# Moving matrix products later in program order in the front of a hybrid attention and retention block

## The chip, the core and the metric

The kernel runs on one core of one Trainium2 chip. The metric is the device time of one execution in microseconds (us). The engines are TensorE (PE in the rows; its weight loads are PEld), VectorE (DVE), ScalarE (ACT), GpSimd (POOL) and SyncE (SP, which issues the transfers).

## What is computed

One layer of an encoder over 1024 rows of 1024 numbers, in float32. Two head groups read the same normalised rows through one projection: windowed attention (8 heads) and retention in both directions (8 heads of width 64, in 8 chunks of 128 rows). Then come an output projection and a gated feed-forward layer. The part that matters here is the retention, cut from the reference:

```python
n = rms_norm(x, attn_norm_w[l])
proj = n @ w_in[l]                        # rq, rk, rv, rg are slices of it
inner = einsum('bhcnd,bhcmd->bhcnm', qc, kc) * dmat
out_inner = einsum('bhcnm,bhcme->bhcne', inner, vc)
kv = einsum('bhcmd,bhcme->bhcde', kc * zeta, vc)
def step(r, kv_c):
    return g_chunk * r + kv_c, r
_, states = lax.scan(step, zeros, kv)     # over the chunks; the other direction flipped
cross = einsum('bhcnd,bhcde->bhcne', qc * xi, states)
ret = rms_norm(fwd + bwd, ret_norm_w)
y_ret = silu(rg) * ret
```

## The kernel before

**Passes and steps.** Each operand of a large product is split into a high and a low part, and three matmuls (`passes`, high by high, high by low, low by high) make one product. In the front a projection is a list `seq` of steps (chunk, row tile, depth slice); `sip()` emits one step, which is three matmuls of 512 columns. A row tile of a chunk has eight steps and one PSUM bank, of which there are three (`MM_BUFS`; the first chunk may take two more). `fill(n)` emits n steps, `need(c, t)` emits steps until tile t of chunk c is complete. Steps are used as filler: the other work of the front waits on VectorE, ScalarE and GpSimd, and the steps put between give TensorE something to do meanwhile. `sip()` also calls for the next weights (a transfer on the SP queue, then a split into high and low by ScalarE and VectorE).

**The loops.** For each of two groups g of four retention heads, first a loop over the eight tiles of keys and values (chunk `A`), then `kv_scan` (the recurrence over chunks, twelve operations on VectorE), then a loop over the eight chunks of queries and gates (chunk `B`). After both come keys and values of the attention (chunk `C`), its queries (`D`), attention, the output projection (`O`) and the feed-forward layer, which the change doesn't touch.

**Keys and values, `kv_phase(g, t, ...)`.** Stage one reads tile t's bank: rotation of the keys, values weighted by the decays (`vz`), and high and low parts of both (`kh`, `kl`, `vh`, `vl`). Stage two is the six matmuls of `a<g><t>pk`, keys by values. Stage three is four copies by ScalarE into `KV`.

**Retention, `ret_phase(g, c, ...)`.** Seven stages, divided by yields:

1. rotation of the queries into `qr` (VectorE; tag `t1`, two buffers) and the gate (ScalarE)
2. four transposes `pt`, then `qkh`, `qkl` and the block-diagonal `bq` (rows `BD<-r..qkh`, `BD<-r..qkl`)
3. `s` (queries by keys, six matmuls), `sd` and `sh`, `c` (queries by states, six matmuls), `sl`, `cx`
4. `i`, the inner products: eight matmuls of 128 columns that read `sh`, `sl` and `vhl`
5. `cx` plus `i`, the sum `Y` of both directions, its square
6. mean of squares (VectorE), reciprocal root `rn` (GpSimd)
7. two products on `Y` (GpSimd); the second reads the gate, which lies in `qr`

`go(gen)` emits one stage, `drain(gen)` all that are left. Between two chunks `states(g, c + 1, ...)` writes the next chunk's states and values.

**Who sets the order.** A planner under the kernel makes the queue of each engine. It takes program order as priority and its own estimate of when operands are ready: if the next instruction in program order isn't ready by that estimate, a later one that is goes first. Once made, each queue runs in its order. Buffers are handed out by tag: a tag with two buffers makes the third tile wait until the first is no longer read.

Lines that the change and the steps below touch: `FILL` (38), `AHEAD` (43), `kv_phase` (stage two at its first yield), `kv_scan`, `states`, `ret_phase`, and the two loops over t and c.

Of the kernel before, what the change touches and what calls it, by code (L numbers as in the profile page):

```python
# [34 lines left out]
       "r_bqh": "a", "r_bql": "ad", "r_sh": "a", "r_sl": "d", "r_y": "d", "r_sq": "a", "r_yn": "p", "r_yg": "p",  # L35
       "q_rope": "d", "k_rope": "d", "q_n": "d", "q_h": "p", "q_l": "dp", "q_T": "a", "p_n": "apap", "p_h": "a",
       "o_c": "a", "o_h": "p", "o_l": "p", "y_h": "a", "m_h": "da"}
FILL = {"A": 2, "Aend": 7, "B1": 2, "B2": 5, "C1": 4, "C2": 4, "D0": 6, "D1": 2, "T1": 3, "O0": 4, "O1": 4, "O2": 3}
SOONER = {"w": -80, "exp": 10, "pass": 0}
EARLY, LATE = (0, 4, 1, 5), (2, 3, 6, 7)  # L40
LEAD = 6
EXTRA = (3, 4)
AHEAD = (7, 7, 6)
DOWN_LEAD = 5
RD_BUFS = 10
FIRST_RAW = 8
# [16 lines left out]
def hymba_block(ctx, tc, x, xT, cst, prm, ffnw, wqkv, wkv, wout, wg, wu, wd, out):  # L63
# [69 lines left out]
    def f32(ap):  # L133
        return ap.bitcast(F32)

    def U(name, tag, dt=F32):
        return up.tile([P, 512], dt, name=name, tag=tag, bufs=SLOTS[tag])
# [4 lines left out]
    def ax_ps(name):  # L142
        return pp.tile([P, 512], F32, name=name, tag="ax", bufs=AX_BUFS)
# [48 lines left out]
    A, B, C, D, O = "a", "b", "c", "d", "o"  # L192
# [57 lines left out]
    def sip():  # L250

        c, t, k = seq[pos[0]]
        per = 2 if c[0] == C else 1
        g = first_granule[c] + k // per
        i = part[0]
        if i == 0:
            while len(W) <= g:
                load_next()
            if c == chunks[0] and t == 0:
                split_x(k, 0)  # L260
            if k == 0:
                banks[c, t] = (ax_ps if c == chunks[0] and t in EXTRA else mm_ps)(f"{c[0]}{c[1]}_{t}")
                begun[0] += 1
        width = 512 // per
        o = (k % per) * width
        lh, ll = (X[:, k, t * P:t * P + P] for X in (X_hi, X_lo))
        rh, rl = (w[:, o:o + width] for w in W[g])
        with sooner("pass"):
            pe.matmul(banks[c, t][:, :width], ll if i == 2 else lh, rl if i == 1 else rh,
                      start=k == 0 and i == 0, stop=k == 7 and i == 2)  # L270
        part[0] = (i + 1) % 3
        if i < 2:
            return
        pos[0] += 1
        if c == chunks[0] and t == 3:
            split_x(k, 1)
        if k == 7:
            done.add((c, t))
        if t == tiles[c][-1] and (k + 1) % per == 0:
            freed[0] = g + 1  # L280
        if not hold[0] and pos[0] % PUMP == 0:
            pump(1)

    def ready():
        if pos[0] >= len(seq):
            return False
        c, t, k = seq[pos[0]]
        if (c[0], t, k // 4) in blocked:
            return False
        return k > 0 or part[0] > 0 or begun[0] - taken[0] < MM_BUFS + (len(EXTRA) if c == chunks[0] else 0)  # L290

    def fill(n):

        n = round(3 * n)
        while n and ready():
            sip()
            n -= 1

    def need(c, t):
        while (c, t) not in done:  # L300
            sip()
        return banks[c, t]

    def took():

        taken[0] += 1
# [14 lines left out]
    def row_rms(t):  # L321
        i = xcount[0] % 8
        xcount[0] += 2
        xv = xs[:, i:i + 2, :]
        nc.sync.dma_start(xv, x[t * P:(t + 1) * P, :].rearrange("p (a c) -> p a c", a=2))
        c = slice(t, t + 1)
        act.activation(xv, xv, AF.Square, accum_out=ssq[:, c])
        dve.tensor_scalar(ssq[:, c], ssq[:, c], 1.0 / DM, EPS, op0=ALU.mult, op1=ALU.add)
        pool.tensor_tensor(rstd[:, c], ssq[:, c], mhalf[:, 0:1], op=ALU.pow)
        dve.tensor_scalar(rstd8[:, c], rstd[:, c], HD ** -0.5, None, op0=ALU.mult)  # L330
        dve.tensor_scalar(e2[:, c], ssq[:, c], EPS * HD, None, op0=ALU.mult)
# [64 lines left out]
    def decay_matrix(g):  # L396

        for fb in range(2):
            for h in range(4):
                hh = 4 * g + h  # L400
                act.activation(dms[:, fb, h, :], ab[:, fb, :], AF.Exp, scale=ld[:, fb, hh:hh + 1])
        dve.tensor_tensor(dms[:, 0], dms[:, 0], dms[:, 1], op=ALU.mult)

    def kv_phase(g, t, ps, kr, rv, KV):

        n = f"a{g}{t}"
        rope(kr, ps[:, 0:256], cosT[:, t, :], sinT[:, t, :], 4, n, rstd8[:, t:t + 1], "a_rope")
        vz = U(f"{n}vz", TAG["vz"])
        vzv = vz[:].rearrange("p (j f q e) -> p j f q e", j=2, f=2, q=2)
        v4 = ps[:, 256:512].rearrange("p (j q e) -> p j q e", j=2, q=2)  # L410
        for fb in range(2):
            z = ze[:, fb, 4 * g:4 * g + 4].rearrange("p (j q) -> p j q", j=2)
            dve.scalar_tensor_tensor(vzv[:, :, fb], v4, rstd[:, t:t + 1], bc(z, 3, HD), op0=ALU.mult, op1=ALU.mult)
        copy("a_rv", rv, ps[:, 256:512], 0, rstd[:, t:t + 1])
        kh, kl = U(f"{n}kh", TAG["kh"], F32R), U(f"{n}kl", TAG["kl"], F32R)
        copy("a_kh", kh[:, :256], kr)
        vh, vl = U(f"{n}vh", TAG["vh"], F32R), U(f"{n}vl", TAG["vl"], F32R)
        copy("a_vh", vh[:], vz[:])
        on("a_kl").tensor_tensor(kl[:, :256], kr, f32(kh[:, :256]), op=ALU.subtract)
        on("a_vl").tensor_tensor(vl[:], vz[:], f32(vh[:]), op=ALU.subtract)  # L420
        yield
        pk = ax_ps(f"{n}pk")
        for j in range(2):
            passes(pk[:, j * 256:j * 256 + 256], kh[:, j * P:j * P + P], kl[:, j * P:j * P + P],
                   vh[:, j * 256:j * 256 + 256], vl[:, j * 256:j * 256 + 256], True, True)
        yield
        pkv = pk[:].rearrange("p (j f q e) -> p j f q e", j=2, f=2, q=2)
        for fb in range(2):
            slot = t if fb == 0 else 7 - t
            if slot == 7:  # L430
                continue
            for par in range(2):
                rows = slice(par * 64, par * 64 + 64)
                copy("a_kv", KV(slot)[rows, fb], pkv[rows, :, fb, par, :], par)
# [90 lines left out]
    def drain(gen):  # L525
        for _ in gen:
            pass

    def go(gen):
        next(gen, None)  # L530
# [3 lines left out]
    old = iter(())  # L534
    for g in range(2):
        kvt = [U(f"KV{g}{i}", "kv") for i in range(4)]
        KV = lambda s: kvt[s // 2][:].rearrange("p (s f j e) -> p s f j e", s=2, f=2, j=2)[:, s % 2]
        krv = [U(f"krv{g}{t}", "kr") for t in range(NT)]
        prev = iter(())
        for t in range(NT):  # L540
            ps = need((A, g), t)
            gen = kv_phase(g, t, ps, krv[t][:, 0:256], krv[t][:, 256:512], KV)
            go(gen)
            took()
            if g == 0 and t + RMS_AHEAD < NT:
                row_rms(t + RMS_AHEAD)
            go(old)
            if g == 0 and t < len(AHEAD):
                fill(AHEAD[t])
            drain(prev)  # L550
            fill(FILL["A"])
            go(gen)
            drain(old)
            if t == LAG_DM:
                decay_matrix(g)
            if g == 0 and t >= 4:
                if t == 4:
                    BD = up.tile([P, 4, DM], F32R, name="BD", tag="b16", bufs=1)
                pool.memset(f32(BD[:, t - 4, :]), 0.0)
            prev = gen  # L560
        drain(prev)
        fill(FILL["Aend"])
        kv_scan(g, KV)
        vhl = U(f"vhl{g}0", TAG["vhl"], F32R)
        states(g, 0, KV, BD, krv[0][:, 256:512], vhl)
        for c in range(NT):
            ps = need((B, g), c)
            if g == 0:
                Y[c] = U(f"Y{c}", "y")
            gen = ret_phase(g, c, ps, krv[c][:, 0:256], vhl, BD, Y[c][:, g * 256:g * 256 + 256])  # L570
            go(gen)
            took()
            go(old)
            fill(FILL["B1"])
            go(gen)
            drain(old)
            fill(FILL["B2"])
            go(gen)
            if c + 1 < NT:
                vhl = U(f"vhl{g}{c + 1}", TAG["vhl"], F32R)  # L580
                states(g, c + 1, KV, BD, krv[c + 1][:, 256:512], vhl)
            go(gen)
            go(gen)
            old = gen


# [78 lines left out]
    def attend(t, kv, qT, yA):  # L665
# [32 lines left out]
        yield  # L698
        fill(FILL["T1"])
        po = ax_ps(f"{n}o")  # L700
# [37 lines left out]
    for t in range(NT):  # L738
        ps = need((C, 0), t)
        gen = key_value(t, ps)  # L740
# [4 lines left out]
        drain(old)  # L745
        fill(FILL["C1"])
        drain(prev)
# [33 lines left out]
    old = iter(())  # L781
    for i in range(2 * NT):
# [18 lines left out]
        old, cur = cur, nxt  # L801
# [216 lines left out]
    for t in EARLY + LATE:  # L1018
# [10 lines left out]
        gen = norm_rows(t, h, (h[0], xr))  # L1029
# [168 lines left out]
```

## Time and profile before

| | us |
|---|---|
| median of 3 runs (lowest to highest) | 1137.11 (1136.93 to 1137.37) |
| the profiled execution, its own time | 1136.94 |
| its span in the trace | 1135.2 |
| TensorE with a matmul under way | 1117.2 |
| VectorE busy | 815.0 |
| ScalarE busy | 573.4 |
| GpSimd busy | 164.8 |

The page gives busy time by engine, the span in 40 slices, the transfers, the chain of work that ended last and the costliest groups. Matmuls are pipelined: the next one starts before the one before it is reported as ended. So lost time on TensorE is best read from the distance between two starts, not from the idle time alone. The front that the change touches ends some 270 us into the span.

### The profile page before, as it was taken

Reading aid. Unit: us, or ns where it says so; the run is one execution under the profiler, and the core shown is the slowest. Engines: PE = TensorE matmul, PEld = TensorE weight load, DVE = VectorE, ACT = ScalarE, POOL = GpSimd, SP = SyncE. Lnnn points to the kernel's source line nnn. Section 1 sums busy time; section 2 is a strip of 40 time slices with the busy share of each in tenths; the row PEclk is TensorE's granted clock in tenths of the full one; section 3 lists DMA queues with packets and bytes.
Section 4 is the critical chain, followed back from the end, with each engine's and each line's share of the span. In section 5 each row is a group of like instructions: output and inputs, shape, how many; then the busy total and the mean of one; then the engine's idle time right before and its main releaser. Section 6 shows DMA issues by size and latency. Waiting matters only on the chain.

```text
span 1135.2 us, 16184 instructions
## 1 busy us (share of the span) xinstructions
PE 1117.2 (98%) x5384; PEld 925.6 (82%) x5384; DVE 815.0 (72%) x1647; ACT 573.4 (51%) x1196; POOL 164.8 (15%) x248
## 2 busy tenths in 40 slices
PE   9999999999999999999999999999999999999998
PEld 7777788789888778788888888888888888888887
DVE  6887857888799997879776577666766655555553
ACT  7954645554589785555333333333333334444441
POOL 1224400444455531000000000000000000000000
PEclk9999999999999999999999999999999999999999
DMA  8520202011100036733554356445544778766681
GB/s 327 183 57 1 75 1 75 1 56 39 38 1 10 20 101 212 240 96 112 176 195 148 114 183 194 141 120 185 188 138 129 261 229 261 248 212 195 218 267 65
DMA packets 84755, 156.53 MB, mean 138 GB/s; under 512 B 9664, under 2 KB 10176, under 8 KB 84672
## 3 DMA queue, kind: packets, MB, share of 16 engines
q1 hardware_dynamic: 84672, 155.51, 42.8%
q8 instruction: 42, 0.69, 0.3%
q14 instruction: 41, 0.34, 0.1%
HBM read 115.36 MB, written 40.11 MB: 137 GB/s over the span
## 4 chain that ended last, share of the span: by engine, by line
PE 83%; DVE 7%; ACT 3%; issue 3%; POOL 3%; DMA 0%; SPq 0%; POOLq 0%; ACTq 0%; DVEq 0%
PE pa L90 21%; PE pc L90 11%; PE da L90 10%; PE pb L90 5%; PE dc L90 5%; PE a L90 5%; PE b L90 5%; PE o L90 4%; PE d L90 3%; PE db L90 3%; PE c L90 1%; POOL Y L90 1%; DVE h L90 1%; ACT KV L90 1%; PE idle L90 0%
## 5 line engine op out<-in xcount | busy, mean ns | idle before, releaser
L90 PE MATMUL b<-wh,X_hi 128*128 128x512 f32 x128 | 51.5, 404 | 0.0
L90 PE MATMUL b<-wh,X_lo 128*128 128x512 f32 x128 | 51.0, 399 | 0.0
L90 PE MATMUL o<-wl,X_hi 128*128 128x512 f32 x128 | 50.4, 396 | 0.6 <-DVE wl L90 0.6
L90 PE MATMUL b<-wl,X_hi 128*128 128x512 f32 x128 | 50.8, 398 | 0.0
L90 PE MATMUL o<-wh,X_hi 128*128 128x512 f32 x128 | 50.7, 397 | 0.0
L90 PE MATMUL a<-wh,X_hi 128*128 128x512 f32 x128 | 50.4, 394 | 0.0
L90 PE MATMUL o<-wh,X_lo 128*128 128x512 f32 x128 | 50.1, 393 | 0.0
L90 PE MATMUL a<-wl,X_hi 128*128 128x512 f32 x128 | 50.0, 392 | 0.0
L90 PE MATMUL a<-wh,X_lo 128*128 128x512 f32 x128 | 49.7, 391 | 0.0
L90 DVE TENSOR_TENSOR S<-A,A 128x512 f32<-128x512 f32 x44 | 30.2, 686 | 1.7 <-DMA A<-in_wg_dram 1.2
L93 DVE TENSOR_TENSOR wl<-raw,wh 128x512 fp32r<-128x512 f32 x44 | 30.6, 711 | 0.1
L90 PEld LDWEIGHTS o<-wl,X_hi 128*128 128x128 f32 x128 | 24.1, 188 | 5.7 <-DVE wl L90 1.4
L90 ACT ACTIVATE sg<-sg 128x512 f32<-128x512 f32 x33 | 20.8, 632 | 15.4 <-DVE sg L90 15.4
L90 PEld LDWEIGHTS a<-wh,X_hi 128*128 128x128 f32 x128 | 24.2, 189 | 4.8
L90 PEld LDWEIGHTS b<-wh,X_lo 128*128 128x128 f32 x128 | 24.3, 190 | 4.6
L90 PEld LDWEIGHTS o<-wh,X_lo 128*128 128x128 f32 x128 | 24.1, 188 | 4.6
L90 PEld LDWEIGHTS b<-wl,X_hi 128*128 128x128 f32 x128 | 24.4, 190 | 4.1 <-DVE wl L93 0.2
L90 PEld LDWEIGHTS a<-wl,X_hi 128*128 128x128 f32 x128 | 24.2, 189 | 4.3
L90 PEld LDWEIGHTS a<-wh,X_lo 128*128 128x128 f32 x128 | 24.0, 188 | 4.4
L90 PEld LDWEIGHTS o<-wh,X_hi 128*128 128x128 f32 x128 | 24.1, 188 | 4.3
L90 DVE TENSOR_TENSOR wl<-raw,wh 128x512 fp32r<-128x512 f32 x32 | 22.0, 718 | 7.4 <-ACT wh L90 7.4
L90 PEld LDWEIGHTS b<-wh,X_hi 128*128 128x128 f32 x128 | 24.3, 190 | 3.6
(2925 smaller groups left out, 3745.5 us busy)
## 6 DMA issues: line engine op xcount, KB each, us to landing
A<-in_wg_dram SPq DMA_DIRECT2D x44, 256.0 KB, 2.8
A<-in_wu_dram SPq DMA_DIRECT2D x44, 256.0 KB, 3.1
R<-in_wd_dram SPq DMA_DIRECT2D x44, 256.0 KB, 2.7
L_S<-LS SPq DMA_DIRECT2D x44, 256.0 KB, 2.3
R_T<-RT SPq DMA_DIRECT2D x44, 256.0 KB, 2.1
raw<-in_wqkv_dram SPq DMA_DIRECT2D x40, 256.0 KB, 3.3
L_A<-a SPq DMA_DIRECT2D x33, 256.0 KB, 2.3
raw<-in_wout_dram SPq DMA_DIRECT2D x32, 256.0 KB, 2.9
```

The costliest lines, as they stand in the source:

```text
L90: ins = fn(*args, **kw)
L93: ins = fn(*args, **kw)
```

## The change

Steps are put in other places, and stages of the retention go to other turns of the loop over chunks.

```diff
-FILL = {"A": 2, "Aend": 7, "B1": 2, "B2": 5, "C1": 4, ...
+FILL = {"A": 6, "Aend": 4, "B1": 3, "B2": 4, "C1": 4, ...
-AHEAD = (7, 7, 6)
+AHEAD = (3, 3, 2)
@@ the loop over tiles t
             go(old)
+            go(old)
             if g == 0 and t < len(AHEAD):
                 fill(AHEAD[t])
             drain(prev)
@@ the loop over chunks c
             go(gen)
             took()
+            fill(FILL["B1"])
             go(old)
-            fill(FILL["B1"])
             go(gen)
+            go(old)
+            fill(FILL["B2"])
             drain(old)
-            fill(FILL["B2"])
             go(gen)
             if c + 1 < NT:
                 vhl = U(f"vhl{g}{c + 1}", TAG["vhl"], F32R)
                 states(g, c + 1, KV, BD, krv[c + 1][:, 256:512], vhl)
-            go(gen)
-            go(gen)
             old = gen
```

In the loop over tiles the products `pk` of a tile stand two steps behind its first stage before the change and six behind it after. For the first three tiles of the first group the sum of steps stays (7 + 2, 7 + 2, 6 + 2 become 3 + 6, 3 + 6, 2 + 6), only the copies of the tile before move ahead.

A turn c of the loop over chunks reads, in program order:

```
before: need(c), 1(c), 6(c-1), 2 steps, 2(c), 7(c-1), 5 steps, 3(c), states, 4(c), 5(c)
after:  need(c), 1(c), 3 steps, 4(c-1), 2(c), 5(c-1), 4 steps, 6(c-1), 7(c-1), 3(c), states
```

The same instructions run in both; only their order is another.

## Rows read from the trace of the kernel before

**Rows 1.** Page, busy us by engine, share of the span, instructions.
```profile
PE 1117.2 (98%) x5384; PEld 925.6 (82%) x5384; DVE 815.0 (72%) x1647; ACT 573.4 (51%) x1196; POOL 164.8 (15%) x248
```
**Rows 2.** TensorE's waits, 40 to 272 us: waiter, releaser, total us, times, longest.
```profile
PE r01i L90 <- ACT r01sh L90: 1.8, 1, 1.8
PE a04pk L90 <- ACT a04vh L90: 1.1, 1, 1.1
PE r07pt L90 <- DVE r07qr L90: 0.6, 1, 0.6
PE r06i L90 <- POOL Y L90: 0.6, 1, 0.6
PE r16i L90 <- POOL Y L90: 0.6, 1, 0.6
PE r01pt L90 <- DVE r01qr L90: 0.6, 1, 0.6
...
PE r11pt L90 <- DVE r11qr L90: 0.3, 1, 0.3
...
PE a03pk L90 <- DVE a03vl L90: 0.3, 1, 0.3
```
**Rows 3.** Timeline of TensorE at one product of keys and values: start us, duration us.
```profile
54.42 0.39 PE L90 MATMUL a<-wl,X_hi 128*128 128x512 f32 x1
54.65 0.39 PE L90 MATMUL a<-wh,X_lo 128*128 128x512 f32 x1
55.48 0.39 PE L90 MATMUL a05pk<-a05vh,a05kh 128*128 128x256 f32 x1 [0.44 <-ACT a05vh L90]
```
**Rows 4.** Timeline of ScalarE ahead of that product.
```profile
52.33 1.13 ACT L90 ACTIVATE KV<-a04pk 64x128 f32<-64x128 f32 x4
53.48 0.42 ACT L90 ACTIVATE a05kh<-krv 128x256 fp32r<-128x256 f32 x1
53.80 0.60 ACT L93 CAST wh<-raw 128x512 fp32r<-128x512 f32 x1
54.43 0.47 ACT L90 ACTIVATE krv<-a,rstd 128x256 f32<-128x256 f32 x1
54.80 0.62 ACT L90 ACTIVATE a05vh<-a05vz 128x512 fp32r<-128x512 f32 x1
```
**Rows 5.** Timeline of TensorE, one turn of the loop over chunks.
```profile
111.01 0.40 PE L90 MATMUL r04s<-BD,r04qkh 128*128 128x256 f32 x2
...
112.45 0.39 PE L90 MATMUL b<-wh,X_hi 128*128 128x512 f32 x1
...
113.38 0.40 PE L90 MATMUL b<-wl,X_hi 128*128 128x512 f32 x1
113.71 0.30 PE L90 MATMUL r04i<-vhl,r04sh 128*128 128x128 f32 x1
113.85 0.45 PE L90 MATMUL b<-wh,X_lo 128*128 128x512 f32 x1
...
115.81 0.38 PE L90 MATMUL r05pt<-ident,r05qr 128*128 128x128 f32 x2
```
**Rows 6.** Timelines of ScalarE, GpSimd (two) and VectorE around the same turns.
```profile
109.91 0.42 ACT L90 ACTIVATE BD<-r04qkl 64x256 fp32r<-64x256 f32 x1
...
118.98 1.01 POOL L90 TENSOR_TENSOR r04rn<-r04ss,mhalf 128x4 f32<-128x4 f32 x1 [1.98 <-DVE r04ss L90]
...
120.77 0.74 POOL L90 TENSOR_TENSOR Y<-Y,r04qr 128x256 f32<-128x256 f32 x1
...
121.86 0.48 DVE L90 SCALAR_TENSOR_TENSOR r06qr<-b,rstd,cosT 128x256 f32<-128x256 f32 x1
```
**Rows 7.** Timeline of VectorE at the wait of the third rotation.
```profile
86.11 0.48 DVE L90 SCALAR_TENSOR_TENSOR r02qr<-b,rstd,cosT 128x256 f32<-128x256 f32 x1 [2.43 <-POOL Y L90]
```
**Rows 8.** Busy us by stretch: PE, PEld, DVE, ACT, POOL, then TensorE's granted clock.
```profile
89.00:92.00 3.00, 3.00 (x13) 2.73 (x12) 2.78 (x7) 1.71 (x4) 1.79 (x3) 0.50 0.00 0
```
**Rows 9.** Timeline of TensorE at the first chunk of the first group.
```profile
76.78 0.36 PE L90 MATMUL r00c<-BD,r00qkh 128*128 128x256 f32 x1 [0.41 <-DVE BD L90]
```
**Rows 10.** Timeline of GpSimd while VectorE splits weights.
```profile
130.80 1.07 POOL L90 TENSOR_TENSOR Y<-Y,r05qr 128x256 f32<-128x256 f32 x1
```

More of the change, by code (lines that the diff above doesn't have):

```diff
@@ L37 @@
        "o_c": "a", "o_h": "p", "o_l": "p", "y_h": "a", "m_h": "da"}
-FILL = {"A": 2, "Aend": 7, "B1": 2, "B2": 5, "C1": 4, "C2": 4, "D0": 6, "D1": 2, "T1": 3, "O0": 4, "O1": 4, "O2": 3}
+FILL = {"A": 6, "Aend": 4, "B1": 3, "B2": 4, "C1": 4, "C2": 4, "D0": 6, "D1": 2, "T1": 3, "O0": 4, "O1": 4, "O2": 3}
 SOONER = {"w": -80, "exp": 10, "pass": 0}
```

## Prediction
> **What bounds the kernel now.** I read the page's busy times first. TensorE has a matmul under way for 98% of the span, 18 us less than all of it [rows 1]. That looks like nothing to gain, but matmuls overlap, so I went on to TensorE's waits in the front and to its timeline, where the distance between starts counts. Four passes between 112.45 and 113.38 start 0.93 / 4 = 0.23 us apart [rows 5]; that is the beat of undisturbed work. A step (three passes) is worth 0.69 us. Where the next start comes later than a beat, TensorE lost time, and since the work on it is the same in both kernels, the change can win only such losses, or add to them.
>
> The waits of the front are short and many. The longest is 1.8 us; then come products of keys and values, inner products and transposes [rows 2]. The view understates them: at 54.65 a pass starts and the product behind it at 55.48, which is 0.83 where 0.23 is the beat, so 0.60 is lost, while the view shows 0.44 [rows 3]. I add that 0.16 to each wait. Behind the longest wait the granted clock is at 0.50, the lower of its two levels (1.2 of 2.4 GHz), for 3 us in which TensorE always had work [rows 8]: 1.5 us more lost.
>
> **The change part by part.**
>
> *Products of keys and values.* Five tiles of the first group wait for their high or low values, a04pk first and a03pk last in the list, 2.5 us in all [rows 2]; with 0.16 each, 3.3 us. The product stands four steps (12 x 0.23 = 2.8 us) further back in program order, and the longest wait is 1.1 + 0.16. What could be late next is the loop through ScalarE: the copies of the tile before (1.13), kh (0.42), a weight split (0.60), the values (0.47) and vh (0.62), 3.24 us in a row from a product's end to the next one's start [rows 4]. Between two products there would be 18 passes, 4.1 us: it fits, with room for one more split of 0.60. With less cover each further split of 0.60 would come back as wait. Taken: -3.0. Bounds: 0, if the planner puts the products where they are, and -4.0, if the passes that now stand between the first product and the other five go too.
>
> The steps that move forward bring their weight loads along (an SP issue, a split on ScalarE and on VectorE each). I cost that at nothing: the same eight blocks are split in the same 20 us, and transfers have no wait in the list of these stretches; the cover is the 0.9 us by which 4.1 exceeds 3.24.
>
> *Scan.* From the last product of a group to the first product with states, program order now has 7 + 2 + 5 = 14 steps and then 4 + 3 + 4 = 11, so 2.1 us less cover, twice. The first such product waits 0.41 for its states already [rows 9]. But the planner draws passes forward where it sees a hole, and up to three tiles' banks are there to draw from. Bounds: 0 and +4.2; taken +0.5, nearest to that one row.
>
> *Inner products in the next turn.* They follow 12 passes behind the state products in place of 4 to 7. r06i and r16i wait 0.6 each, with 0.16 more 1.5 together [rows 2]; eight passes more are 1.8 us each, so both go: -1.5. r01i loses 1.8 + 0.16; five passes more (12 in place of 7) cover 1.15 of it, and with a shorter hole I count half of the slow clock [rows 8], 0.75: -1.9. Bounds for this part: 0 and -5.0.
>
> *Transposes.* In the turn shown, the rotated queries' transpose starts 3.36 us behind the state products; nine passes take 2.07 of that, the rest 1.29 [rows 5]. With twelve passes ahead it is 2.76 + 1.29 less 0.13 (next item) = 3.92, so 0.56 later relative to the rotation. r07pt, r01pt and r11pt wait 0.76, 0.76 and 0.46 with the 0.16 [rows 2]; 0.56, 0.4 and 0.46 of it covered: -1.4. Bounds 0 and -2.0.
>
> *One group of inner products in place of two.* Now the first inner product stands alone between passes: it starts 0.33 behind a pass and the next pass 0.14 behind it [rows 5], against 0.23 and (by the same row) some 0.11 to 0.14 each, so about 0.13 goes for the break in each of some twelve turns: up to -1.6. Taken -0.8, since the planner may break the group again.
>
> *What comes closer.* (a) From transposes to s there are four steps in place of five. The last part of bq ends at 110.33 and s starts at 111.01 [rows 5, 6]: 0.68 of margin, one step 0.69. So the margin is gone but nothing is owed: 0; if another ScalarE copy of 0.42 [rows 6] comes first, up to +0.42 x 14 = +5.9. (b) The rotation of chunk c writes the buffer that the last product on Y of chunk c-2 reads. Now that product ends at 121.51 and the rotation starts at 121.86 [rows 6], 0.35 apart. The inner products end one step later less the 0.13, so 0.56; the rotation then waits 0.2, or 0.6 if the square goes behind one more copy of 0.42. Behind it on VectorE's queue stand the next sl, sums and rotations, which the transposes wait for, and they have the 0.56 of the item before. Taken +0.1 in each of 12 turns, +1.2; bounds 0 and +0.4 x 12 = +4.8.
>
> Sum: -3.0 + 0.5 - 1.5 - 1.9 - 1.4 - 0.8 + 0 + 1.2 = -6.9. On the profiled execution, 1136.94, that gives 1130.0; it lies 0.17 under the median of the runs shown, which I neglect. All favourable bounds together (4.0 + 5.0 + 2.0 + 1.6, the slow clock gone as a whole) would give 1136.94 - 12.6 = 1124.3; half of the gains would give about 1133.5. The forecast's own range is 1124 to 1134.
>
> **The rivals.**
>
> *The planner has done it already.* In the turn shown five passes stand between the state products and the first inner product although program order has none there [rows 5]. If program order hardly decides where a product lands, waits stay where the estimate misses the chip. For: the same row. Against: the products stand where they just miss their operands, which is what priority over passes does, and passes with higher priority would stand ahead of them. Time: 1136.9.
>
> *The scan takes it back.* The upper bound of the scan item, +4.2, and no gain at r01i, which hangs on the same turns: -3.0 + 4.2 - 1.5 - 1.4 - 0.8 + 1.2 = -1.3, so 1135.6. For: states are already late [rows 9]. Against: up to three banks of passes to draw on.
>
> *The two buffers of qr become the bound; slower.* This has happened once in the trace: the rotation of the third chunk stood 2.43 us on VectorE for a product on Y [rows 7], the score's multiplication queued behind it, and TensorE's 1.8 us wait and the slow clock followed. After the change, that product comes later by 0.56, by 0.42 for the square, and by 0.33 where it runs as the one of 1.07 did beside VectorE's weight splits in place of 0.74 [rows 6, 10]; if the mean of squares also queues behind a rotation and two more copies, another 0.7. That is 2.0 late against 0.35 + 0.56 of cover, 1.1 per turn. The point from which it decides is 0.6 per turn, since 14 turns of that take the gains of 8.6. At 1.1 it is 15.4 - 8.6 = +6.8: 1143.7. Against: in most turns VectorE has idle time and the product on Y takes 0.74.
>
> The Trainium skill speaks for this rival (SBUF — State Buffer, "Who interferes with whom"): a VectorE instruction with two inputs in SBUF contends with a GpSimd instruction that reads SBUF. The 1.07 in place of 0.74 [rows 6, 10] agrees. By that rule the products on Y, which move from beside s and c to beside the rotations and sums, would take the 0.33 in every turn, 4.6 us over 14 if all of it reached TensorE; by the rows it is taken as covered in most.
>
> **How the numbers follow.** About 0.2% (2.3 us) is what a measurement of this kernel can tell from no change. Forecast 0.66, at 1130.0; planner 0.14; scan 0.07; buffers 0.13. Faster takes nearly all of the forecast and a little of the scan's spread (its upper term is a bound): 0.68. Same takes the planner, most of the scan: 0.19. Slower takes the buffers: 0.13. The range that should hold 8 in 10 runs from 1123 (just under all favourable bounds) to 1138.5, which takes in the planner and the scan and leaves out the buffers.
>
> **What would show it.** Right: no wait of a kv product over 0.3 in the first group; r06i and r16i out of TensorE's list; inner products as one group of eight behind some twelve passes; no stretch at half clock between 85 and 95. The kv item is wrong if ScalarE's chain of 3.24 is longer than the passes between two products. The scan item is wrong if r00c or r10c waits over 1 us. The buffers have become the bound if VectorE's waits list rotations (r..qr) behind GpSimd's Y in most turns. The prediction as a whole is wrong if the waits of the front sum to as much as now, or if the stages behind 270 us, which run the same program, change by more than 1 us.

## The result and the profile after

| | before | after |
|---|---|---|
| median, us (lowest to highest) | 1137.02 (1136.56 to 1137.37, 4 runs) | 1147.72 (1145.11 to 1147.94, 4 runs) |
| the profiled execution, its own time | 1136.94 | 1147.94 |
| its span in the trace | 1135.2 | 1146.1 |

The ratio is 1.009, with a 95% interval of 1.0078 to 1.0103: the changed kernel is some 11 us slower, where 6.9 us less was forecast.

The page's busy line, the same columns as [rows 1], shows hardly a difference.

```profile
PE 1117.9 (98%) x5384; PEld 929.8 (81%) x5384; DVE 822.7 (72%) x1647; ACT 572.6 (50%) x1196; POOL 163.7 (14%) x248
```

TensorE has 0.7 us more "busy" and the span is 10.9 longer; the share rounds to 98% both times. So I measured every distance between two starts on TensorE and took off the beat of the columns in it (0.226 us for 512, 0.174 for 384, 0.119 for 256, 0.058 for 128, each from undisturbed stretches). What is left over is lost time. By stretch, in us:

| | keys and values, group 0 (a03pk to a07pk) | chunks, group 0 (r01pt to r07pt) | chunks, group 1 (r11pt to r17pt) | everything else | sum |
|---|---|---|---|---|---|
| before | 4.3 | 11.4 | 7.3 | 43.8 | 66.8 |
| after | 1.2 | 22.0 | 10.2 | 44.4 | 77.8 |

The sums differ by 11.0, the spans by 10.9: nothing is missing from this account. (About 0.45 us in each turn over the chunks is no wait: the eight inner products start 0.11 us apart, as most products of 128 columns do, where those of the attention's transposes take 0.058.) The products of keys and values gained 3.1. The loop over chunks lost 10.6 in the first group and 2.9 in the second.

TensorE's waits from 40 to 285 us (waiter, releaser, total us, times, longest), the counterpart of [rows 2]:

```profile
PE r06i L90 <- DVE r06sl L90: 1.7, 1, 1.7
PE r05s L90 <- ACT BD L90: 1.7, 1, 1.7
PE r16s L90 <- ACT BD L90: 1.4, 1, 1.4
PE r02i L90 <- issue: 1.3, 1, 1.3
PE r03i L90 <- issue: 1.3, 1, 1.3
PE r11i L90 <- ACT r11sh L90: 1.3, 1, 1.3
PE r01i L90 <- ACT r01sh L90: 1.3, 1, 1.3
PE r05i L90 <- DVE r05sl L90: 1.2, 1, 1.2
```

The first group's products `pk` are gone from the view, and so are most transposes `pt`. In their place the inner products `i` of chunks 1 to 6 of the first group wait (of the second, those of 1, 6 and 7), and some score products `s`, r05s and r16s most. VectorE's waits in the same stretch say why:

```profile
DVE r03qr L90 <- POOL Y L90: 2.6, 1, 2.6
```

The same line stands there for r02qr, r04qr, r05qr and r12qr, 2.6 us each, and shorter ones for r06qr, r07qr and r17qr (1.2, 1.4 and 0.6). Before, one rotation waited like that, 2.43 [rows 7]. VectorE's timeline at one of them (start us, duration us, operation, in brackets the idle time ahead of it and what ended it):

```profile
94.58 0.17 DVE L90 TENSOR_SCALAR r01ss<-r01ss 128x4 f32<-128x4 f32 x1
97.40 0.48 DVE L90 SCALAR_TENSOR_TENSOR r03qr<-b,rstd,cosT 128x256 f32<-128x256 f32 x1 [2.65 <-POOL Y L90]
97.80 0.68 DVE L90 TENSOR_TENSOR r02sd<-r02s,dms 128x512 f32<-128x512 f32 x1
...
102.58 0.69 DVE L90 TENSOR_TENSOR r02cx<-r02cx,r02i 128x512 f32<-128x512 f32 x1
...
105.14 0.17 DVE L90 TENSOR_SCALAR r02ss<-r02ss 128x4 f32<-128x4 f32 x1
```

GpSimd meanwhile:

```profile
94.83 1.02 POOL L90 TENSOR_TENSOR r01rn<-r01ss,mhalf 128x4 f32<-128x4 f32 x1 [2.99 <-DVE r01ss L90]
95.93 0.61 POOL L90 TENSOR_TENSOR Y<-Y,r01rn 128x256 f32<-128x256 f32 x1
96.63 0.74 POOL L90 TENSOR_TENSOR Y<-Y,r01qr 128x256 f32<-128x256 f32 x1
```

ScalarE and TensorE behind it:

```profile
98.52 0.63 ACT L90 ACTIVATE r02sh<-r02sd 128x512 fp32r<-128x512 f32 x1 [2.32 <-DVE r02sd L90]
```
```profile
97.52 0.39 PE L90 MATMUL b<-wh,X_lo 128*128 128x512 f32 x1
99.24 0.30 PE L90 MATMUL r02i<-vhl,r02sh 128*128 128x128 f32 x1 [1.33 <-issue]
```

Read them together. The rotation of chunk 3 stands *ahead* of `sd` of chunk 2 on VectorE's queue. It writes the buffer of `qr` that chunk 1 used, and the last reader of that buffer is GpSimd's second product on `Y`, because the gate lies in it; that ends at 97.37. So `sd` starts at 97.80, `sh` at 98.52, and the inner products at 99.24, 1.72 behind the last pass. From the rotation on VectorE works without a break, through `sd`, `cx` plus `i` and the sum `Y` of chunk 2 to its mean of squares, which ends at 105.31: 7.9 us. Only then can GpSimd start chunk 2's root and its two products on `Y`, 2.6 us, and the rotation of chunk 4 waits for the last of them. The loop closes over **one** turn and runs through VectorE and GpSimd: the rotations of chunks 3, 4 and 5 start at 97.40, 107.94 and 118.48, 10.54 apart each time. TensorE has to follow: its distance from one chunk's transposes to the next is 10.5 us (starts 90.3, 100.8, 111.4 and 121.9 for chunks 2 to 5), where 8.47 were taken before (107.10 to 115.57). Its late inner products show the loop but don't set its length: the last of chunk 2 ends at 101.0, and VectorE comes to `cx` plus `i` at 102.58, behind work of its own.

Before, the rotation stood behind `sd`, so that GpSimd's 2.6 us ran beside `sd` and `cx`, and the loop would close only over two turns. VectorE's timeline before:

```profile
103.47 0.69 DVE L90 TENSOR_TENSOR r03sd<-r03s,dms 128x512 f32<-128x512 f32 x1 [1.47 <-PE r03s L90]
...
104.95 0.48 DVE L90 SCALAR_TENSOR_TENSOR r04qr<-b,rstd,cosT 128x256 f32<-128x256 f32 x1
```

What puts the rotation there is how far the passes run ahead. I counted on TensorE's timeline the passes of queries and gates that started ahead of chunk c's transposes and took off the 24 for each chunk up to c:

| passes ahead at the transposes of chunk | 0 | 1 | 2 | 3 | 4 | 5 |
|---|---|---|---|---|---|---|
| before | 9 | 15 | 7 | 6 | 6 | 6 |
| after | 45 | 42 | 39 | 36 | 33 | 30 |

More passes follow between the transposes and `s`. Where the count reaches 24 by then, the *next* chunk's bank is complete, and its rotation has everything it reads before `s` of this chunk has run. Counted at `s`, turns 0 and 1 of the first group have 24 before and the later ones 21; after, turns 0 to 5 have 57 falling to 42, turn 6 has 24, and the second group starts with 27 and 24 and goes on with 21. The reversed order stands on VectorE's queue in turns 0 to 4 of the first group (the rotations of chunks 1 to 5) and 0 and 1 of the second after, and in turns 0 and 1 of the first before. No turn with 21 has it; not every turn with 24 or more does. (In turns 5 and 6 after, the rotation stands between `sd` and `sl` and waits there.)

### The profile page after: what moved, and what is told of

It is laid out like the page before. It is cut to its first block, busy times and chain, and to the rows that moved or that the text cites. A ratio compares the mean times of both kernels' runs of the same rounds, so it can differ in the third digit from the quotient of the medians.

```text
span 1146.1 us, 16171 instructions
## 1 busy us (share of the span) xinstructions
PE 1117.9 (98%) x5384; PEld 929.8 (81%) x5384; DVE 822.7 (72%) x1647; ACT 572.6 (50%) x1196; POOL 163.7 (14%) x248
## 4 chain that ended last, share of the span: by engine, by line
PE 78%; DVE 8%; issue 5%; POOL 4%; ACT 3%; DMA 0%; SPq 0%; POOLq 0%; ACTq 0%; DVEq 0%
PE pa L90 21%; PE pc L90 10%; PE da L90 10%; PE pb L90 5%; PE dc L90 5%; PE o L90 4%; PE a L90 4%; PE d L90 3%; PE b L90 3%; PE db L90 3%; POOL Y L90 1%; PE c L90 1%; POOL vhl L90 1%; DVE h L90 1%; ACT wh L93 0%
## 6 DMA issues: line engine op xcount, KB each, us to landing
A<-in_wg_dram SPq DMA_DIRECT2D x44, 256.0 KB, 2.8
A<-in_wu_dram SPq DMA_DIRECT2D x44, 256.0 KB, 3.1
R<-in_wd_dram SPq DMA_DIRECT2D x44, 256.0 KB, 2.7
L_S<-LS SPq DMA_DIRECT2D x44, 256.0 KB, 2.3
R_T<-RT SPq DMA_DIRECT2D x44, 256.0 KB, 2.1
raw<-in_wqkv_dram SPq DMA_DIRECT2D x40, 256.0 KB, 2.9
L_A<-a SPq DMA_DIRECT2D x33, 256.0 KB, 2.3
raw<-in_wout_dram SPq DMA_DIRECT2D x32, 256.0 KB, 2.8
```

## The experiments

The suspects were the two halves of the change (keys and values; retention), the buffer that holds the gate, the lead of the passes, and ScalarE's queue ahead of `s`. Ratios are against runs of the kernel before on the same chip (medians 1136.74 to 1137.11).

**One half at a time.** The first kernel is the one before with only the fill numbers of keys and values changed.

```diff
-FILL = {"A": 2, "Aend": 7, ...
+FILL = {"A": 6, "Aend": 4, ...
-AHEAD = (7, 7, 6)
+AHEAD = (3, 3, 2)
```

> Only the part on keys and values is done (steps A 6, Aend 4, AHEAD 3, 3, 2); the turns of the chunk loop are those of before. In its VectorE queue the rotation of chunk c+1 stands ahead of chunk c's score multiplication sd in six turns of the first group and two of the second, as in five and two with the whole change. Theory L (the lead of passes puts the rotation ahead of sd, where it waits for the two buffers): slower than before by 3 to 10 us, with waits of r..qr for Y of about 2.4 us in several turns. Rival I (the late inner products are the cause): the kv waits of 3.3 us go and nothing else comes, 1133 to 1135.

Measured: 1146.21, ratio 1.0084 (1.0067 to 1.0101). The half that was to win 3 us costs 9. The old order of the retention stages doesn't protect from the loop: VectorE's waits, 60 to 285 us, have the same five lines of 2.6 us as after, and a longer one for r06qr (1.2 after).

```profile
DVE r03qr L90 <- POOL Y L90: 2.6, 1, 2.6
...
DVE r06qr L90 <- POOL Y L90: 1.8, 1, 1.8
```

The second is the kernel after with these numbers put back, so that only the retention stages are moved.

```diff
-FILL = {"A": 6, "Aend": 4, ...
+FILL = {"A": 2, "Aend": 7, ...
-AHEAD = (3, 3, 2)
+AHEAD = (7, 7, 6)
```

> Only the turns of the chunk loop are changed (inner products in the next turn, B1 3, B2 4, two stages of the old chunk in the loop over tiles); the steps of the kv loop are those of before. The rotation stands ahead of sd in one turn only. Theory L: the turns run at some 8.25 us without new waits, 2 to 6 us faster than before, 1131 to 1135. Rival I: waits of inner products for sh as with the whole change, 1143 to 1148.

Measured: 1135.76, ratio 0.9992 (0.9983 to 1.0001), 12, 15, 9 and 9 passes ahead at the transposes of chunks 0 to 3. No loss, and nearly no gain, 0.8 short of the range expected: the moved stages are harmless alone. The two halves make +9.2 and -1.3, together +10.7; the 2.8 left over are hardly more than the three intervals allow, so that the two halves make each other worse isn't shown.

**The gate out of `qr`.** If the loop is the cause, the gate's place is what closes it. The gate can lie where the chunk's values were, in the upper half of `krv`, which is free by then:

```diff
-    def ret_phase(g, c, ps, kr, vhl, BD, yv):
+    def ret_phase(g, c, ps, kr, vhl, BD, yv, gw):
-        gw = qr[:, 256:512]
...
-            gen = ret_phase(..., Y[c][:, g * 256:g * 256 + 256])
+            gen = ret_phase(..., Y[c][:, g * 256:g * 256 + 256], krv[c][:, 256:512])
```

> The whole change, but the gate is written into the values' half of krv (dead after states) in place of the second half of qr, so that a rotation waits only for the transposes two chunks back and not for GpSimd's last product. The VectorE order still has the rotation ahead of sd in seven turns and two. Theory G (the two buffers of qr are what the early rotation waits for): no wait of r..qr for Y, 1126 to 1132. If the early place of the rotation costs by itself: 1140 to 1148.

Measured: 1132.95, ratio 0.9967 (0.9954 to 0.998), 1.0 above the range expected. No rotation waits for `Y` any more, though it still stands ahead of `sd`, now in all seven turns of the first group. VectorE's timeline:

```profile
92.94 0.47 DVE L90 SCALAR_TENSOR_TENSOR r04qr<-b,rstd,cosT 128x256 f32<-128x256 f32 x1
93.65 0.69 DVE L90 TENSOR_TENSOR r02sd<-r02s,dms 128x512 f32<-128x512 f32 x1 [0.15 <-PE r02s L90]
```

Here chunk 4's rotation runs before chunk 2's `sd` and does no harm, since nothing makes it wait. The place in the queue alone doesn't bring the loss; with the wait taken away 14.8 us are won. TensorE's waits from 80 to 135 us still list `s`, though:

```profile
PE r05s L90 <- ACT r04cx L90: 1.3, 1, 1.3
PE r06s L90 <- ACT r05cx L90: 1.2, 1, 1.2
PE r03s L90 <- ACT BD L90: 0.7, 1, 0.7
PE r02s L90 <- ACT BD L90: 0.5, 1, 0.5
```

**The lead taken away, the buffer left.** The kernel after, with fewer steps emitted ahead around the keys and values:

```diff
-FILL = {"A": 6, "Aend": 4, ...
+FILL = {"A": 6, "Aend": 0, ...
-AHEAD = (3, 3, 2)
+AHEAD = (0, 0, 0)
```

> The whole change with twelve steps fewer ahead of the first chunk loop (AHEAD 0, 0, 0 and Aend 0; the kv products stay six steps back). The rotation stands ahead of sd in one turn only. Theory L: both gains are there, no waits of r..qr over 1 us but for one turn, 1127 to 1133; the shorter cover of the scan may add 1 to 2. Rival I (late inner products): 1143 to 1148.

Measured: 1135.3, ratio 0.9987 (0.9977 to 0.9996); 9, 16, 9 and 9 passes ahead at the transposes of chunks 0 to 3, and the reversed order in one turn instead of seven. With gate and stages where the changed kernel has them, the loss is gone. That is the other way to open the loop. It is still 2.3 above the range expected; the waits at keys and values came partly back (a04pk 1.0, a03pk and a05pk 0.4 each), and the planner left 14 to 17 passes from one product's first matmul to the next one's where program order has 18. Why it did isn't settled.

**The same move of the gate in each of the other orders.** Three kernels: the one before, the one with keys and values alone, and the one with retention alone, each with the gate in `krv`, by the edit above.

> The kernel before, with the gate moved out of qr alone. In it the rotation stands ahead of sd in two turns of the first group, and one of them waited 2.43 us for Y. Theory G: that wait, r01i's 1.8 us and the slow clock behind it go, the rest stays: 2 to 3.5 us faster than before, 1133.5 to 1135. If the buffers matter only with late inner products: 1136 to 1137.

> The kernel before with the kv part of the change and with the gate moved out of qr; the turns of the chunk loop are those of before. Theory L and G: the kv gain of 3.1 and that of the gate alone add up, 1130 to 1132.5, although the rotation stands ahead of sd in seven turns; against the 1146 of the kv part alone the two buffers then cost about 15 us. If the lead costs by another way too: over 1136.

> The turns of the change on the kernel before, gate moved, kv steps of before. Against e5 (1133.88, gate moved alone) it shows what late inner products are worth when the buffers don't hold them. By the forecast's terms for inner products, transposes and unbroken groups without r01i (1.5 + 1.0 + 0.8): 1130 to 1131.5. If s with four steps of cover takes that back: 1133 to 1135.

Measured medians in us, with those from above:

| | gate in `qr` | gate in `krv` |
|---|---|---|
| neither half (before) | 1137.02 | 1133.88, ratio 0.9971 (0.996 to 0.9982) |
| keys and values | 1146.21 | 1134.56, ratio 0.998 (0.9971 to 0.9989) |
| retention stages | 1135.76 | 1132.94, ratio 0.9964 (0.9952 to 0.9977) |
| both (after) | 1147.72 | 1132.95, ratio 0.9967 (0.9954 to 0.998) |

The buffer cost the kernel before 3.1 us already. With it out of the way the retention half is worth 0.9, which the intervals don't tell from nothing; it comes out 1.4 behind what I had expected of it. The half of keys and values is worth nothing in this column (1134.56 is 2.1 above the range expected), although its waits are gone: lost time by stretch, in the order of the first table, is 4.3, 8.0, 6.6, 43.6 for retention with the gate moved, and 1.2, 11.5, 7.3, 42.6 for both. Three microseconds won among keys and values are lost again among the chunks. The e12 kernel below was made for that.

**More delay in the loop.** The kernel after, with GpSimd's root computed twice in a row (the same result; 1.0 us more each time):

```diff
         pool.tensor_tensor(rn[:], ss[:], mhalf[:, :4], op=ALU.pow)
+        pool.tensor_tensor(rn[:], ss[:], mhalf[:, :4], op=ALU.pow)
```

> The whole change with the reciprocal root of each chunk computed twice on GpSimd (1.0 us more there, 16 times; the same result). Theory G: GpSimd's part of the loop from one chunk's inner products to the next one's lies on the path of the turns whose rotation waits for Y (r02 to r05, r12, and in part r06 and r07): 1.0 us each there, 4 to 8 us slower than the whole change, 1152 to 1156. If GpSimd isn't on the path: 1147 to 1149.

Measured: 1160.88, ratio 1.021 (1.0195 to 1.0225), 13.2 us more than after, for sixteen roots of 1.0 us. I had expected 4 to 8: only the locked turns were to pay. In those the delay comes through whole: the rotations of chunks 3, 4 and 5 start 11.61 and 11.62 apart, where 10.54 were taken after. And it locks other turns too. VectorE's waits, 60 to 285 us:

```profile
DVE r02qr L90 <- POOL Y L90: 3.7, 1, 3.7
DVE r12qr L90 <- POOL Y L90: 3.7, 1, 3.7
DVE r07qr L90 <- POOL Y L90: 2.5, 1, 2.5
```

3.7 where 2.6 stood, longer waits for r06qr and r07qr, and new ones for the rotations of chunks 3 to 6 of the second group (0.8 to 1.6), where the turns of chunks 3 to 5 take 9.23 to 9.26 in place of 8.25. By the account of the first table (for the profiled execution) the two loops over chunks lose some 6 and 4.5 us more than after, and the rest of the kernel 4. GpSimd is busy for 14% of the span, and yet its time is paid where it stands in this loop.

**More passes behind, or the square on another engine, with the gate moved.** Three tries at the waits that e3 left at `s` and `i`. The first gives back the old split of steps (2 and 5), the others move the square from ScalarE to GpSimd, for both halves and for keys and values alone:

```diff
-"B1": 3, "B2": 4,
+"B1": 2, "B2": 5,
```

> The kernel of e3 with two steps ahead of the inner products and five between transposes and s (B1 2, B2 5) in place of three and four. Theory S: what kept e3 behind the forecast is s waiting for the last copy into bq, which stands behind the square on ScalarE (0.5 to 1.3 us in six turns); one step more is 0.69, so most of those waits go, 2 to 4 us faster than e3, 1129 to 1131. If the square itself is late because of VectorE, the wait moves with it: same as e3 within 1 us.

```diff
-"r_sq": "a",
+"r_sq": "p",
```

> The kernel of e3 (whole change, gate moved) with the square of Y on GpSimd in place of ScalarE. Theory S: s waits because the last copy into bq stands on ScalarE behind that square, which itself waits for VectorE; with the square elsewhere the copy runs at once, the waits of r02s to r06s, r11s, r12s (0.5 to 1.3 us, some 6 us in all with 0.16 each) go for the most part: 1127 to 1130. If s would wait for VectorE's part of bq anyway: 1132 to 1134.

> The kernel of e6 (kv part, gate moved, turns of before) with the square on GpSimd. There only r05s and r06s wait for s, and r05i once: theory S gives 1 to 3 us less than e6, 1131.5 to 1133.5; no gain, if those waits are VectorE's weight splits, 1134 to 1135.

Measured: 1134.68, ratio 0.998 (0.9971 to 0.999); 1132.58, ratio 0.9961 (0.9949 to 0.9974); 1136.35, ratio 0.9995 (0.9986 to 1.0004). All three missed what I expected (1129 to 1131, 1127 to 1130, 1131.5 to 1133.5). The first moved the waits of chunks 2 to 4 from `s` to `i`; 2 and 5 is the same sum as 3 and 4, seven steps a turn. In the second, TensorE's waits from 80 to 135 us show the same products late for the next engine:

```profile
PE r05s L90 <- DVE BD L90: 1.1, 1, 1.1
PE r06s L90 <- DVE BD L90: 1.1, 1, 1.1
...
PE r03s L90 <- DVE BD L90: 0.2, 1, 0.2
```

Before `r05s` ScalarE was late, now VectorE is, and 0.2 us of 1.3 came off; r02s to r04s fell from 1.7 in sum to 0.6. Three turns took 7.98, 7.99 and 7.98 where e3 has 8.34, 8.67 and 8.52, so the square's place is part of what sets them; but the 1.4 us won in the first group are lost again behind it, and the medians differ by 0.4. What is short as well is work for TensorE to do meanwhile: each turn emits seven steps, 21 passes, while a chunk needs 24. Three turns of e3, from one chunk's transposes to the next (stretch, its length, then busy us and count of PE, PEld, DVE, ACT and POOL, the clock, DMA share, GB/s):

```profile
88.74:97.08 8.34, 7.84 (x48) 6.67 (x47) 7.95 (x18) 4.41 (x10) 4.55 (x7) 1.00 0.00 0
97.08:105.75 8.67, 8.01 (x47) 6.66 (x47) 8.37 (x18) 4.41 (x10) 4.28 (x7) 1.00 0.01 3
105.75:114.27 8.52, 8.03 (x48) 6.67 (x47) 7.84 (x17) 5.09 (x12) 4.13 (x7) 1.00 0.00 1
```

and for two of e11, whose passes run 9 ahead at the transposes, where those of e3 run 39 to 33:

```profile
95.50:103.75 8.25, 8.25 (x50) 7.25 (x50) 7.19 (x18) 4.30 (x10) 4.80 (x6) 1.00 0.01 4
103.75:112.00 8.25, 8.25 (x50) 7.25 (x50) 7.18 (x18) 4.29 (x10) 4.85 (x7) 1.00 0.00 0
```

e11 has 24 passes in a turn of 8.25 and TensorE is never idle. e3 has 47 or 48 matmuls in place of 50 (those on an edge of the stretch count as well), three passes or 0.68 us less to do, and its turns take as long or longer. So passes taken ahead came back as holes. The holes needn't come from the missing passes alone: VectorE is busy for 7.84 to 8.37 us of e3's turns and for 7.2 of e11's. The difference is mainly a pair of operations `BD<-KV,BD`, which takes 1.46 us in e3 and 0.65 in e11.

**Eight steps a turn.** The e3 kernel, and then the kernel after, with one step more in each turn, so that the lead is kept instead of used up:

```diff
-"B1": 3, "B2": 4,
+"B1": 3, "B2": 5,
```

> The kernel of e3 with five steps in place of four between transposes and s, eight a turn and so as many as a tile has (B1 3, B2 5). Theory H: the 3.1 us that the kv loop gained come back as holes, since passes that ran there are missing in the turns, which have 21 passes in place of 24 and can't be shorter than some 8.3 us. With 24 in each turn the holes of r02 to r06 (0.65 to 1.4 each) close: 1129 to 1131, if what is left of the lead finds cover later, and about 1133 if the attention stage gives it back. If VectorE sets the turns' length whatever the passes: the turns get no holes but get longer by 0.69 each, 1132 to 1134.

> The whole change with eight steps a turn (B1 3, B2 5), the gate left in qr. Theory G: the turns whose rotation waits for Y are set by a loop of some 10.4 us from one chunk's inner products to the next, which three passes more can't shorten. Now the lead lasts, so that more turns are of that kind (all 14 by VectorE's order): 14 turns of 10.4 in place of 8.25 are 30 us, less the clock: 1146 to 1160. If the 21 passes a turn were the whole cause: 1127 to 1132, as with the gate moved.

Measured, with the gate in `krv`: **1126.38**, ratio 0.9906 (0.9889 to 0.9922), the fastest of all and 2.6 below the range expected, which had counted on the first group alone. The lead stays at 45 passes through chunk 5, and TensorE's timeline shows an unbroken turn, inner products 0.23 behind a pass:

```profile
89.44 0.41 PE L90 MATMUL r02pt<-ident,krv 128*128 128x128 f32 x2
...
96.61 0.40 PE L90 MATMUL b<-wh,X_lo 128*128 128x512 f32 x1
96.84 0.23 PE L90 MATMUL r02i<-vhl,r02sh 128*128 128x128 f32 x1
...
97.69 0.41 PE L90 MATMUL r03pt<-ident,krv 128*128 128x128 f32 x2
```

A turn is 97.69 - 89.44 = 8.25, the same as in e11, and the lost time is 1.2, 7.0, 5.7 and 42.4. Here the gain of keys and values is kept: the first number stays at 1.2 and the second isn't worse for it. (VectorE is back at 7.2 us a turn too, so the eighth step may have helped by its passes or by shifting VectorE's work; the runs don't part the two.) With the gate left in `qr`: 1150.43, ratio 1.0122 (1.0105 to 1.0139). The same lead that pays in e12 costs here: the loop now holds for ten chunks, five of each group, and the turn shown takes 10.53 us.

```profile
226.12 0.41 PE L90 MATMUL r13pt<-ident,krv 128*128 128x128 f32 x2
...
233.38 0.39 PE L90 MATMUL b<-wh,X_lo 128*128 128x512 f32 x1
235.07 0.30 PE L90 MATMUL r13i<-vhl,r13sh 128*128 128x128 f32 x1 [1.31 <-issue]
...
236.65 0.41 PE L90 MATMUL r14pt<-ident,krv 128*128 128x128 f32 x2
```

The place of the gate is all that differs, and 24 us lie between these two kernels.

## Why the prediction was wrong

**The step that failed** is (b), "The rotation of chunk c writes the buffer that the last product on Y of chunk c-2 reads": taken +1.2, with +4.8 as its bound. The buffer was right, the price was not. Moving the gate out of the buffer wins 14.8 us in the kernel after and 3.1 in the kernel before, so the change made the buffer 11.6 us dearer. The step priced the wait with the rotation in the place it has in [rows 6], behind everything of the chunk before. It didn't ask what the other half of the change does to that place: with 45 passes ahead in place of 9, the planner has the bank of chunk c+1 ready before `s` of chunk c and puts the rotation ahead of `sd`. (That it goes by its estimate of readiness is argued from how it works; the place itself is read from the queue, and e2 and e4 show that it goes with the lead.) In that place the wait isn't 0.2 or 0.6 but 2.6, the whole of GpSimd's root and products, since what these read is the last thing that VectorE makes ahead of the rotation.

This isn't the whole miss. With the gate in `krv` on both sides the change is worth 0.9 (1133.88 to 1132.95, within the noise), where the forecast's other terms came to 8.1. So they were too large by some 7 us: the gain among keys and values was given back in the turns, that of the inner products didn't come, and step (a), put at nothing, cost something (below).

**Where the working went past it.** Two things were in my hands. [rows 7] had shown the full wait, 2.43, with the score's multiplication queued behind it, as I wrote myself; I took it for an event of the start, though the kernel before has it at just those chunks where the lead is largest (15 passes at chunk 1). And the item on keys and values asked of the moved steps only whether their weight loads are hidden, not what becomes ready early on other engines' queues.

**The rival** with the two buffers had the mechanism, and its time of 1143.7 comes nearer to 1147.7 than the forecast, in part by luck: its trigger was wrong. It took the product on `Y` to come two microseconds later, in part by contention. In the turns after that waited, that product takes 0.72 to 0.74 and the one ahead of it 0.61 or 0.62, as in undisturbed turns before [rows 6]; the 1.07 of [rows 10] isn't what makes the wait. So the rule of the Trainium skill (SBUF — State Buffer, "Who interferes with whom"), which spoke for this rival, agrees with the 1.07 but didn't decide the wait here. What did take longer is VectorE's pair `BD<-KV,BD`, 1.46 in the turns of 10.54 for 0.65 before, while GpSimd works on `BD` and `vhl`; in e12 it takes 0.76 beside the same two operations, so the cause of that isn't settled. Nor was 0.13 a fair chance for a loop that the trace had shown once.

The other steps, in turn:

| step | taken, us | measured |
|---|---|---|
| keys and values | -3.0 | -3.1 in their own stretch (4.3 to 1.2) |
| weight loads moved along | 0 | +0.4, two new waits of a pass for `wl` |
| scan | +0.5 | about 0: the wait at r00c is gone, r10c has 0.5 |
| inner products in the next turn | -3.4 | didn't come: r01i, r06i and r16i still wait, 1.8, 1.7 and 0.7 |
| transposes | -1.4 | right in kind: of the three, none waits; r17pt has 0.3 |
| one group of inner products | -0.8 | about -0.2 a turn where nothing waits: 8.25 for 8.46 |
| (a) one step less ahead of `s` | 0 | 0.5 in r02s and r03s, up to 1.7 in r05s; with the gate moved (e3) 0.5 to 1.3 in r02s to r06s |
| (b) buffers of `qr` | +1.2 | 11.6, by the kernels with the gate moved |

*Keys and values*: right, and the row is TensorE's timeline at the place of [rows 3].

```profile
56.31 0.40 PE L90 MATMUL b<-wh,X_lo 128*128 128x512 f32 x1
56.55 0.28 PE L90 MATMUL a05pk<-a05vh,a05kh 128*128 128x256 f32 x1
```

The product starts 0.24 behind a pass, not 0.83. What I didn't foresee is that the gain isn't kept: e3 against e11 shows it given back in turns with three passes too few, and e12 shows it kept as soon as the turns have them.

*Step (a)*: the zero came from a margin of 0.68 against a step of 0.69, and the bound of +5.9 from one more ScalarE copy ahead of the last part of `bq`. That copy is there, the square:

```profile
93.20 0.42 ACT L90 ACTIVATE r01cx<-Y 128x256 f32<-128x256 f32 x1 [0.80 <-DVE Y L90]
93.81 0.42 ACT L90 ACTIVATE BD<-r02qkl 64x256 fp32r<-64x256 f32 x1 [0.18 <-DVE r02qkl L90]
```

and TensorE starts `r02s` late for it:

```profile
94.27 0.39 PE L90 MATMUL r02s<-BD,r02qkh 128*128 128x256 f32 x1 [0.50 <-ACT BD L90]
```

It had its cause named and its size open; the value between the ends was the wrong one.

*The planner*, the first rival, was half right in a way that I hadn't priced: program order decides less than the banks of passes that lie ready. It had been costed as "no change".

*What would make the prediction wrong*: it named "VectorE's waits list rotations (r..qr) behind GpSimd's Y in most turns", and that is what the trace after lists, in 8 of 14 turns. Everything outside the three stretches of the first table, the stages behind the front included, lost 0.6 us more in sum (44.4 for 43.8): no part of the cause lies there.

Two things stay open: what in all sets the 8.3 to 8.7 us of e3's turns (the square on ScalarE is a part, VectorE's fuller turn perhaps another), and why e4's planner put fewer passes between the products than program order has.

## What to carry to other kernels

Filler moved ahead isn't only cover: it makes the next stage's operands ready early, and where something orders queues by readiness, the early stage goes ahead of the late one and takes its waits along; so for each step moved forward, ask what becomes ready sooner, on which queue it lands, and which buffer it must wait for there. A wait seen once, with something of the critical chain queued behind it, is to be followed round: if the chain it delays ends in its own releaser, every turn in which that order occurs becomes as long as the loop (10.5 us for 8.5 here). And work taken ahead of a loop can leave holes in the loop unless each turn puts back as much as it uses (24 passes, not 21): on the kernel before, the gate's move alone gave 3 us; the whole change with the gate moved and the eighth step gave 10.7.

## What the runs showed of the hardware

TensorE's granted clock fell to 0.50, the lower of its levels (1.2 of 2.4 GHz), in more places than before [rows 8]. The stretches after (columns as in the windows above):

```profile
112.30:115.50 3.20, 3.20 (x9) 2.46 (x8) 3.07 (x6) 1.98 (x5) 0.63 (x1) 0.50 0.00 0
143.00:146.20 3.20, 3.20 (x13) 2.91 (x13) 2.54 (x6) 1.75 (x4) 0.00 (x0) 0.50 0.00 0
221.50:224.70 3.20, 3.20 (x9) 2.42 (x9) 3.08 (x5) 2.15 (x5) 0.92 (x2) 0.50 0.00 0
```

Three of them where the kernel before had one, each behind waits at `i` or `s`. In the account of the first table they come to some 5.1 us, against 1.7 before. That they make the kernel longer isn't shown: the rotations of chunks 4 and 5, with the stretch at 112.30 between them, start 10.54 apart, as those of chunks 3 and 4 do at full clock. Where a turn waits for VectorE and GpSimd anyway, slower passes cost nothing. And the kernel after ran in 1147.68 with a mean granted clock of 0.999, in 1147.77, 1147.94 and 1145.11 with 0.996. Where no such loop holds the turn, the stretch does cost: in the series of runs beside the experiments, the kernel before took 1136.05 (median of 24 runs) with a mean granted clock of 1.000 and 1137.20 (47 runs) with 0.998, so about 1.2 us for the one stretch, where the forecast had 1.5. With the root doubled there were eight stretches. Of the kernels with the gate moved, the one with `B1` 2 and `B2` 5 had one (252.6 to 256.0), the others none in the front.

Also unexpected: the root of 128x4 numbers takes GpSimd 1.02 us, longer than its products of 128x256 (0.61 and 0.74). The Trainium skill says of TensorE that matmul busy time "is a bad metric, because matmuls are pipelined" (Perfetto Trace Analysis, the note at its head); the trace agrees, 98% both before and after with 10.9 us between the spans, and the distances between starts found all of it.
